# Mean squares of the attention heads by halves of the tokens, and sums of the second weights spread over eight pairs

## The chip, the cores and the metric

The kernel runs on one core of one Trainium2 chip. The metric is the device time of one execution in microseconds (us); before the change the median of three runs is 1240.09 us (1237.65 to 1240.2). A core has TensorE (PE; its weight loads are the rows PEld), VectorE (DVE), ScalarE (ACT), GpSimd (POOL) and SyncE (SP), whose queue issues all DMAs of this kernel in program order.

## What is computed

One layer over 1024 tokens of width 1024 in float32: layer norm, attention without softmax over 8 heads with a decay along the keys, beside it four groups of pooled projections; head outputs are scaled by their root mean square, joined with the pooled groups, projected and added to the residual; then a feed-forward layer of squared ReLU and a per-layer embedding. The part that matters here, in short:

```python
o = o * rsqrt(mean(o * o, per head) + eps) * head_scale   # heads, in pairs
mixed = concat(heads, pooled) ; x = x + mixed @ w_out
h = relu(norm(x) @ w_up) ** 2 ; x = x + h @ w_down
```

## The kernel before

Products of float32 precision are made of three matmuls, high by high, low by high and high by low (L69 to L71); L65 casts to the high part and L66 subtracts for the low one. Tags name the buffers in SBUF that tiles share; a tile that asks for a tag waits until the older tile's last reader is done.

**Attention** goes over 64 tiles: 4 pairs of heads (`pr`) by 2 heads (`j`) by 8 row tiles (`t`). For a tile, `weigh` makes the scores `z` (L396, L397), ACT writes `rr` and `aa` from them, DVE scans (L400), POOL adds (L403); `turn` transposes `aa` (L126), ACT and DVE split it into `ath` and `atl`, and `gather`, after every second tile, multiplies by the values into `o` (L429). `weigh` runs three tiles ahead of `turn`. Between them `fill` puts matmuls of the later projections (`pq`) and of the pooled groups (`pp`), at a rate `RATES[0]` up to tile 48 and `RATES[1]` from it; what is left comes in `fill.finish`. PE's order is the order of the code here; the other engines are ordered by a scheduler.

After the last tile of a pair `rms_square` squares the pair's whole output `oraw` (L441), `rms_stats` multiplies it by `hm` into `pm` (L447), ACT adds eps (L450), POOL raises it to the power of −1/2 (L451) and copies it to `ms` (L453); `rms_apply` transposes a half of it into `pb` (L460) and DVE multiplies `oraw` by it (L462). For pairs 0 to 2 `oraw` is then stored to DRAM (`mspill`); so are pooled groups 5 to 7.

**Out-projection.** `mix(k)` takes the eight inputs in the order 7, 6, 5, 4, 0, 1, 2, 3; six of them come back from `mspill` as `mraw`, 4 is the pooled group in SBUF and 3 the last pair's `oraw`. Each is split and used by the matmuls `acc<-wh,mix`. `wraw` is a row block of `w_out`, `wh` and `wl` its parts, `xr` the residual rows.

**Up stage.** Two hidden blocks make a pair `g`, of 16, computed as two by two blocks with seven products p1 to p7 of 12 matmuls each. Here all engines follow the order of the code, `for g in range(NG)`: p3 of a pair, then p6, p5, p7, and p1 and p2 of the next pair between. `up_load(g, f)` loads half f of the pair's first weights (`uraw`), of which DVE and ACT make sums, highs and lows (`s`, `uh`, `ul`; L574, L655).

The sums of the second weights, for the stage after, are made on the side: `down_fetch(m)` loads two raw blocks of `w_down` (`draw`, 512 KB each), `down_sums(m)` subtracts four times on POOL (L574), `down_out(m)` stores four results of 256 KB (`tspill`). The two buffers are reused, so the loads for m + 1 wait in SP's queue until the stores of m have landed, and stores wait there for the subtractions; all that is queued behind them waits too. `hidden_out` stores the results of the products (`hspill`). Before the change block m was summed at the start of pair g (m = g up to pair 3, g + 1 after it), and stored behind p7, with the loads of m + 1 right after; pair 3 summed and stored block 4 as well, at its end.

Of the kernel before, what the change touches and what calls it, by code (L numbers as in the profile page):

```python
# [8 lines left out]
F32 = mybir.dt.float32  # L9
# [7 lines left out]
P = 128  # L17
# [17 lines left out]
def hymba_layer(ctx: ExitStack, tc: tile.TileContext, x, p, emb_g, emb_b, w_in, attn_g, w_pool,  # L35
# [327 lines left out]
    V.tensor_copy(out=diag[:, S - P:S], in_=ident)  # L363
    oraw = {}

    RATES = (0.37, 0.6)
    AHEAD = 3

    def head_values(pr, j):
# [66 lines left out]
        V.tensor_tensor(out=oraw[k.pr][rows[k.j], (k.t - 1) * P:(k.t + 1) * P],  # L436
                        in0=o[0:HD, 0:2 * P], in1=ob, op=ALU.add)

    def rms_square(pr):
        sq[pr] = slot("ra", "sq")  # L440
        A.activation(out=sq[pr], in_=oraw[pr], func=AF.Square)  # L441

    def rms_stats(pr):

        pm = bank("b6", "pm")[:, 0:2 * NT]
        for i in range(NT):
            T.matmul(pm[:, 2 * i:2 * i + 2], lhsT=sq[pr][:, i * P:(i + 1) * P], rhs=hm,  # L447
                     start=True, stop=True)
        rs = small.tile([P, 2 * NT], F32, name="rms", bufs=2)
        A.activation(out=rs, in_=pm, func=AF.Identity, bias=eps)  # L450
        G.tensor_tensor(out=rs, in0=rs, in1=mhalf, op=ALU.pow)  # L451
        ms[pr] = slot("K", "ms")
        G.tensor_copy(out=ms[pr].rearrange("p (n d) -> p n d", d=HD),  # L453
                      in_=rs.unsqueeze(2).broadcast_to([P, 2 * NT, HD]))

    def rms_apply(pr, c):
        cs = slice(c * CH, (c + 1) * CH)
        pb = bank("b6", "pb")
        for i in range(4):
            T.transpose(pb[:, i * P:(i + 1) * P],  # L460
                        ms[pr][:, (4 * c + i) * P:(4 * c + i + 1) * P], ident)
        V.scalar_tensor_tensor(out=oraw[pr][:, cs], in0=oraw[pr][:, cs],  # L462
                               scalar=osc[:, pr:pr + 1], in1=pb, op0=ALU.mult, op1=ALU.mult)
        if pr < 3 and c:
            load(mspill[pr], oraw[pr])
# [56 lines left out]
    with tc.manual_schedule(engines={mybir.EngineType.PE}):  # L522
        for n in range(-AHEAD, len(tiles)):
            if n >= 0:
                k = tiles[n]
                turn(k)
            if n + AHEAD < len(tiles):
                ahead = tiles[min(n + AHEAD + 1, len(tiles) - 1)]
                if ahead.j == 0 and ahead.t % 4 == 0:
                    fill.until((ahead.pr, ahead.t // 4))  # L530
                weigh(tiles[n + AHEAD])
            fill.rate = RATES[0] if n < 48 else RATES[1]
            if n < 0:
                fill.run(3)
            else:
                fill.share(k.n / P + 1.5)
                if k.t % 2:
                    gather(k)
                for f, *args in later.pop(n, ()):
                    f(*args)  # L540
                if k.j == 1 and k.t == NT - 1:
                    rms_square(k.pr)
                    later.setdefault(n + 2, []).append((rms_stats, k.pr))
                    later.setdefault(n + 8, []).append((rms_apply, k.pr, 0))
                    later.setdefault(n + 10, []).append((rms_apply, k.pr, 1))
        fill.run(4)
        rms_stats(3)
        fill.finish()
        rms_apply(3, 0)
        rms_apply(3, 1)  # L550


    mixh, mixl = {}, {}
# [3 lines left out]
    def mix(k):  # L557
        both = big("mix")
        mixh[k], mixl[k] = both[:, 0:S], both[:, S:2 * S]
        raw = pooled[0] if k == 4 else oraw[3] if k == 3 else None  # L560
        if raw is None:
            raw = slot("K", "mraw")
            load(raw, mspill[k])
        split(raw, mixh[k], mixl[k])
# [375 lines left out]
    def beside(s, n):  # L940
        plan = (PLAN if s else FIRST).get(n, ())
        for what, nx, j, q in plan:
            if s + nx < NS:
                acts[what](s + nx, j, q)

    with tc.manual_schedule(engines=ALL):

        stats, tps = {}, {}
# [89 lines left out]

        for g in range(NG):
            n1, n2 = g + 1 if g + 1 < NG else None, g + 2 if g + 2 < NG else None  # L1040

            m = g if g < 4 else g + 1
            if g:
                up(g, "p6")
                keep(g, "a21")
# [4 lines left out]
                    lows[n1, 0]()  # L1050
            if n1:
                up_load(n1, 1)
                down_sums(m)
            else:
                for i in range(3):
                    fetch_rows(i)
                down_load(0, 1, 0)
# [5 lines left out]
                hidden_out(g - 1, 1)  # L1063
            if n2:
                up_load(n2, 0)
            if not n1:
                down_high(0, 0, 0)
                down_load(0, 1, 1)
# [4 lines left out]
            if g:  # L1073
                hidden_sums(g - 1, 1)
                hidden_out(g - 1, 2)
            if m < NG:
                down_out(m)
            if m + 1 < NG:
                down_fetch(m + 1)
            if not n1:  # L1080
                down_low(0, 0, 0)
                relu2(quarter(g, "a22"))
# [2 lines left out]
            if n1:  # L1085
# [2 lines left out]
                    keep(n1, "a11")  # L1088
                relu2(quarter(g, "a22"))
                up_s21(n1)  # L1090
                if g:
                    up(n1, "p2")
                    take(n1, "a11", "C")
                up_s21_high(n1)
                if not n2:
                    for q in range(2):
                        down_load(0, 0, q)
# [2 lines left out]
            relu2(quarter(g, "a12"), ups[g, "A"])  # L1100
            hidden_out(g, 0)
            hidden_out(g, 3)
            if g == 3:
                down_sums(4)
            if n1:
                if g:
                    relu2(quarter(n1, "a11"))
# [13 lines left out]
            else:  # L1121
# [1 line left out]
                down_high(0, 1, 1)  # L1123
                fetch_rows(3)
                down_load(0, 2, 0)
            if g == 3:
                down_out(4)
                down_fetch(5)

        for s in range(NS - 1):  # L1130
            for n, (name, t) in enumerate(SEQ):
# [200 lines left out]
```

## Time and profile before

| | us |
|---|---|
| median of three runs | 1240.09 |
| profiled execution | 1238.67 |
| its span | 1236.7 |

| engine | busy us | share of the span |
|---|---|---|
| PE | 1163.7 | 94% |
| DVE | 903.1 | 73% |
| ACT | 599.2 | 48% |
| POOL | 520.3 | 42% |

In windows by stretch a row holds the stretch, its length and, for PE, PEld, DVE, ACT and POOL, busy time with the number of instructions; then the granted clock of PE (1.00 is 2.4 GHz, 0.50 is 1.2 GHz), the busy share of the DMA engines and GB/s. A timeline row holds the start, the duration of one or of the grouped instructions together, the engine, line, operation, output<-input, count and, in brackets, idle time before it and who ended it. SPq is SP's queue: a row there is the issue of a DMA, not its transfer.

### The profile page before, as it was taken

How to read it: one execution, taken by the hardware profiler on the slowest of the kernel's cores; microseconds unless marked ns; L12 is line 12 of the kernel's file. 1: busy time of each engine (PE TensorE's matmuls, PEld its weight loads, DVE VectorE, ACT ScalarE, POOL GpSimd, SP SyncE). 2: the span in 40 equal slices, each digit the busy share in tenths (PEclk: the TensorE clock that was granted, in tenths of full speed). 3: DMA queues.
4: the chain of work that ended last, by engine and by line, in shares of the span. 5: the costliest groups of instructions: out<-in, count | busy, mean ns of one | idle time of the engine just before them, and what ended most of it. 6: DMA issues, size and time to landing. Idle time of an engine off the chain costs nothing.

```text
span 1236.7 us, 15529 instructions
## 1 busy us (share of the span) xinstructions
PE 1163.7 (94%) x5520; PEld 964.1 (78%) x5520; DVE 903.1 (73%) x1114; ACT 599.2 (48%) x1038; POOL 520.3 (42%) x368
## 2 busy tenths in 40 slices
PE   7999988899997998699899999999999999998997
PEld 5877877787876876588688888878888888887886
DVE  7735878796865678868576776768888887788565
ACT  5425756675644244454446455466333343335653
POOL 3211443354752236633342332336645564465332
PEclk9999999999997999799899999999999999999999
DMA  9824121121226363378778877799666655643122
GB/s 347 291 115 136 27 61 60 43 60 43 71 83 242 120 243 132 102 253 263 238 256 278 269 252 261 253 378 394 231 220 196 214 175 169 208 138 118 68 78 76
DMA packets 123580, 221.48 MB, mean 179 GB/s; under 512 B 9456, under 2 KB 64240, under 8 KB 123504
## 3 DMA queue, kind: packets, MB, share of 16 engines
q1 hardware_dynamic: 123504, 220.50, 52.4%
q8 instruction: 43, 0.70, 0.2%
q14 instruction: 33, 0.27, 0.1%
HBM read 148.12 MB, written 70.25 MB: 177 GB/s over the span
## 4 chain that ended last, share of the span: by engine, by line
PE 71%; DVE 10%; ACT 6%; DMA 5%; issue 5%; POOL 2%; SPq 1%; DVEq 0%; ACTq 0%; POOLq 0%
PE pd L69 8%; PE pd L71 7%; PE pd L70 7%; PE pu L70 6%; PE pu L71 6%; PE pu L69 6%; PE tp L126 3%; PE pq L69 3%; PE pq L70 3%; PE pq L71 2%; PE acc L70 2%; PE o L429 2%; DVE rr L400 2%; PE acc L71 2%; PE acc L69 2%
## 5 line engine op out<-in xcount | busy, mean ns | idle before, releaser
L574 POOL TENSOR_TENSOR draw<-draw 128x512 f32<-128x512 f32 x64 | 97.1, 1517 | 180.1 <-DMA draw<-in_w_down_dram 177.5
L890 DVE TENSOR_TENSOR xres<-xres,pd 128x512 f32<-128x512 f32 x208 | 137.4, 680 | 45.4 <-PE pd L71 44.5
L574 POOL TENSOR_TENSOR dop<-draw,dop 128x1024 fp32r<-128x1024 f32 (+1 forms) x48 | 112.1, 2355 | 125.2 <-ACT dop L866 107.1
L866 ACT CAST dop<-draw 128x1024 fp32r<-128x1024 f32 (+1 forms) x96 | 81.3, 905 | 134.8 <-DVE xres L890 51.4
L69 PE MATMUL pd<-dop 128*128 128x512 f32 x320 | 125.1, 391 | 2.0 <-DVE xres L890 1.9
L70 PE MATMUL pd<-dop 128*128 128x512 f32 x320 | 124.8, 390 | 0.1
L71 PE MATMUL pd<-dop 128*128 128x512 f32 x320 | 124.6, 389 | 0.0
L574 DVE TENSOR_TENSOR dop<-draw,dop 128x1024 fp32r<-128x1024 f32 (+1 forms) x48 | 85.6, 1784 | 3.6 <-ACT dop L866 3.6
L751 ACT COPY hid<-pu 128x512 f32<-128x512 f32 x48 | 28.2, 588 | 120.8 <-PE pu L71 69.0
L69 PE MATMUL pq<-xh,wh 128*128 128x512 f32 x192 | 77.9, 406 | 0.8 <-DVE ul L66 0.8
L400 DVE TENSOR_TENSOR_SCAN rr<-rr,diag 128x640 f32<-128x640 f32 (+3 forms) x32 | 71.3, 2228 | 9.5 <-ACT rr L398 8.6
L403 POOL TENSOR_TENSOR aa<-aa,rr 128x639 f32<-128x639 f32 (+3 forms) x32 | 56.9, 1779 | 48.4 <-DVE rr L400 48.4
L70 PE MATMUL pq<-xl,wh 128*128 128x512 f32 x192 | 76.7, 399 | 0.0
L71 PE MATMUL pq<-xh,wl 128*128 128x512 f32 x192 | 76.5, 398 | 0.0
L69 PEld LDWEIGHTS pd<-dop 128*128 128x128 f32 x320 | 60.0, 188 | 16.6 <-DVE xres L890 3.2
L574 DVE TENSOR_TENSOR hid<-pu,hid 128x512 f32<-128x512 f32 x48 | 33.0, 688 | 52.7 <-PE pu L71 37.8
L70 PEld LDWEIGHTS pd<-dop 128*128 128x128 f32 x320 | 60.1, 188 | 13.0 <-POOL dop L574 0.8
L71 PEld LDWEIGHTS pd<-dop 128*128 128x128 f32 x320 | 60.1, 188 | 12.5
L65 ACT CAST wh<-wraw 128x1024 fp32r<-128x1024 f32 x36 | 38.0, 1056 | 53.9 <-PE acc L70 26.2
L66 DVE TENSOR_TENSOR atl<-tp,ath 128x512 fp32r<-128x512 f32 (+2 forms) x96 | 50.7, 546 | 15.4 <-ACT ath L65 14.6
L70 PE MATMUL acc<-wl,mix 128*128 128x512 f32 x128 | 51.7, 404 | 4.2 <-POOL wl L66 4.2
L574 DVE TENSOR_TENSOR hid<-hid,hid 128x512 f32<-128x512 f32 x48 | 53.8, 1145 | 0.6
(253 smaller groups left out, 3359.3 us busy)
## 6 DMA issues: line engine op xcount, KB each, us to landing
hspill<-hid SPq DMA_DIRECT2D x48, 512.0 KB, 4.9
draw<-hspill SPq DMA_DIRECT2D x48, 512.0 KB, 6.0
uraw<-in_w_up_dram SPq DMA_DIRECT2D x32, 512.0 KB, 5.8
draw<-in_w_down_dram SPq DMA_DIRECT2D x32, 512.0 KB, 4.7
tspill<-draw SPq DMA_DIRECT2D x64, 256.0 KB, 4.2
wraw<-in_w_out_dram SPq DMA_DIRECT2D x24, 512.0 KB, 3.6
draw<-in_w_down_dram SPq DMA_DIRECT2D x48, 256.0 KB, 5.1
wraw<-in_w_in_dram SPq DMA_DIRECT2D x16, 512.0 KB, 4.9
```

The source lines that it names most:

```text
L65: A.copy(out=h, in_=src)
L66: (eng or V).tensor_tensor(out=l, in0=src, in1=h.bitcast(F32), op=ALU.subtract)
L69: T.matmul(ps, lhsT=lh, rhs=rh, start=start, stop=False, **kw)
L70: T.matmul(ps, lhsT=lh, rhs=rl, start=False, stop=False, **kw)
L71: T.matmul(ps, lhsT=ll, rhs=rh, start=False, stop=stop, **kw)
L126: T.transpose(tp[:, j * P:(j + 1) * P], src[:, (k0 + j) * P:(k0 + j + 1) * P], ident)
L400: V.tensor_tensor_scan(out=rr[:, 0:n][:, ::-1], data0=rr[:, 0:n][:, ::-1], data1=diag[:, S - n:S][:, ::-1], initial=0.0, op0=ALU.mult, op1 ...
L403: G.tensor_tensor(out=aa[:, 0:n - 1], in0=aa[:, 0:n - 1], in1=rr[:, 1:n], op=ALU.mult)
L574: eng.tensor_tensor(out=o, in0=i0, in1=i1, op=op)
L751: A.copy(out=quarter(g, name), in_=ups[g, "A"])
L866: A.copy(out=h, in_=raw)
L890: V.tensor_tensor(out=xres[i][:, cs], in0=xres[i][:, cs], in1=src, op=ALU.add)
```

## The change

There are two edits that share no code. In attention the squares, their means and their use are made by halves of the tokens: half 0 of a pair after row tile 3 of its second head, half 1 after row tile 7, each 1, 2 and 4 tiles later; before, the whole pair was squared at once and its means taken two tiles later, and used eight and ten tiles later. `RATES[1]` goes from 0.6 to 0.8. For the last pair, `mix(3)` splits the two halves apart and applies half 1 just before its split. In the up stage `weight_sums(g, n)` is called at seven steps of every pair: block m is summed at step 6m (up to block 7) or 7(m − 1) and stored, with the next loads, three steps later, so that block 7 is summed at the start of pair 6 and from there the places are as before.

```diff
-    RATES = (0.37, 0.6)
+    RATES = (0.37, 0.8)
...
-    def rms_square(pr):
-        sq[pr] = slot("ra", "sq")
-        A.activation(out=sq[pr], in_=oraw[pr], func=AF.Square)
...
+    def half(c):
+        return slice(c * CH, (c + 1) * CH)
+
+    def rms_square(pr, c):
+        if pr not in sq:
+            sq[pr], ms[pr] = slot("ra", "sq"), slot("K", "ms")
+        A.activation(out=sq[pr][:, half(c)], in_=oraw[pr][:, half(c)], func=AF.Square)
+
+    def rms_stats(pr, c):
+
+        pm = bank("b6", "pm")[:, 0:NT]
+        for i in range(4):
+            T.matmul(pm[:, 2 * i:2 * i + 2], lhsT=sq[pr][:, (4 * c + i) * P:(4 * c + i + 1) * P],
+                     rhs=hm, start=True, stop=True)
...
+        G.tensor_tensor(out=rs, in0=rs, in1=mhalf[:, 0:NT], op=ALU.pow)
+        G.tensor_copy(out=ms[pr][:, half(c)].rearrange("p (n d) -> p n d", d=HD),
+                      in_=rs.unsqueeze(2).broadcast_to([P, NT, HD]))
...
-                if k.j == 1 and k.t == NT - 1:
-                    rms_square(k.pr)
-                    later.setdefault(n + 2, []).append((rms_stats, k.pr))
-                    later.setdefault(n + 8, []).append((rms_apply, k.pr, 0))
-                    later.setdefault(n + 10, []).append((rms_apply, k.pr, 1))
-        fill.run(4)
-        rms_stats(3)
+                if k.j == 1 and k.t in (3, 7):
+                    c = k.t // 4
+                    for m, f in ((1, rms_square), (2, rms_stats), (4, rms_apply)):
+                        later.setdefault(n + m, []).append((f, k.pr, c))
         fill.finish()
-        rms_apply(3, 0)
-        rms_apply(3, 1)
+        for n in sorted(later):
+            for f, *args in later[n]:
+                if f is not rms_apply:
+                    f(*args)
...
+        if k == 3:
+
+            for c in range(2):
+                if c:
+                    rms_apply(3, 1)
+                split(oraw[3][:, half(c)], mixh[k][:, half(c)], mixl[k][:, half(c)])
+            return
...
+    sums_at = {6 * m if m < 8 else 7 * (m - 1): m for m in range(NG)}
+
+    def weight_sums(g, n):
+        n += 7 * g
+        if n in sums_at:
+            down_sums(sums_at[n])
+        if n - 3 in sums_at:
+            m = sums_at[n - 3]
+            down_out(m)
+            if m + 1 < NG:
+                down_fetch(m + 1)
...
-            m = g if g < 4 else g + 1
...
-                down_sums(m)
+                weight_sums(g, 0)
...
-            if m < NG:
-                down_out(m)
-            if m + 1 < NG:
-                down_fetch(m + 1)
+            weight_sums(g, 2)
...
-            if g == 3:
-                down_sums(4)
...
-            if g == 3:
-                down_out(4)
-                down_fetch(5)
+            weight_sums(g, 6)
```

PE's order from the last `z` on, just before the gather of row tiles 60 and 61 to the first `acc`. A triple of `pq` or `pp` is one step of fill. Before, the last gather and what stands behind it:

```order
L429 MATMUL o<-ath,vs 128x256 x7
L429 MATMUL o<-ath,vs 128x128
L429 MATMUL o<-atl,vs 128x128
L429 MATMUL o<-atl,vs 128x256 x7
L69 MATMUL pq<-xh,wh 128x512
L70 MATMUL pq<-xl,wh 128x512
L71 MATMUL pq<-xh,wl 128x512
L69 MATMUL pp<-uh,wph 128x512
L70 MATMUL pp<-ul,wph 128x512
L71 MATMUL pp<-uh,wpl 128x512
...
L447 MATMUL pm<-hm,sq 128x2 x8
L460 MATMUL pb<-ident,ms 128x128 x8
```

and now, with the gather of tiles 60 and 61 ahead of it:

```order
L429 MATMUL o<-atl,vs 128x256 x5
L451 MATMUL pm<-hm,sq 128x2 x4
L126 MATMUL tp<-ident,aa 128x128 x15
L429 MATMUL o<-ath,vs 128x256 x7
L429 MATMUL o<-ath,vs 128x128
L429 MATMUL o<-atl,vs 128x128
L429 MATMUL o<-atl,vs 128x256 x7
L462 MATMUL pb<-ident,ms 128x128 x4
L69 MATMUL acc<-wh,mix 128x512
```

The last fill triple stood three triples behind the last gather and now stands ahead of the gather before it: of the 23 triples behind the last `z` (20 of them ahead of the last gather) 10 are left, and 13 more stand ahead of that `z`. `pm` of half 1 and its `pb` now stand among the `acc` matmuls.

SP's queue at the same place, before:

```order
L74 DMA wraw<-in_w_out_dram 128x1024
L74 DMA mspill<-pooled 128x1024
L74 DMA xr<-xspill 128x1024 x3
L74 DMA mspill<-pooled 128x1024
L74 DMA xr<-xspill 128x1024
L74 DMA uraw<-in_w_up_dram 128x8x128
L74 DMA wraw<-in_w_out_dram 128x1024
L74 DMA mraw<-mspill 128x1024 x6
```

and now:

```order
L74 DMA uraw<-in_w_up_dram 128x8x128
L74 DMA mspill<-pooled 128x1024
L74 DMA wraw<-in_w_out_dram 128x1024
L74 DMA mraw<-mspill 128x1024 x6
L74 DMA xr<-xspill 128x1024 x4
L74 DMA uraw<-in_w_up_dram 128x8x128
```

The six `mraw` loads have passed the four `xr` loads and one `uraw`; one `wraw` still stands right ahead of them.

SP's queue in pairs 2 and 3 of the up stage, from the first half of pair 4's first weights to the second half of pair 5's, before:

```order
L74 DMA uraw<-in_w_up_dram 128x8x128
L74 DMA hspill<-hid_5132 128x1024
L74 DMA tspill<-draw 128x512 x4
L74 DMA draw<-in_w_down_dram 128x1024 x2
...
L74 DMA uraw<-in_w_up_dram 128x8x128
L74 DMA hspill<-hid_5261 128x1024
L74 DMA uraw<-in_w_up_dram 128x8x128
L74 DMA hspill<-hid_5281 128x1024
L74 DMA tspill<-draw 128x512 x4
...
L74 DMA tspill<-draw 128x512 x4
L74 DMA draw<-in_w_down_dram 128x1024 x2
L74 DMA uraw<-in_w_up_dram 128x8x128
```

and now:

```order
L74 DMA uraw<-in_w_up_dram 128x8x128
L74 DMA tspill<-draw 128x512 x4
L74 DMA draw<-in_w_down_dram 128x1024 x2
...
L74 DMA hspill<-hid_5114 128x512
L74 DMA uraw<-in_w_up_dram 128x8x128
L74 DMA tspill<-draw 128x512 x4
L74 DMA draw<-in_w_down_dram 128x1024 x2
L74 DMA hspill<-hid_5295 128x1024
L74 DMA uraw<-in_w_up_dram 128x8x128
...
L74 DMA tspill<-draw 128x512 x4
L74 DMA draw<-in_w_down_dram 128x1024 x2
L74 DMA uraw<-in_w_up_dram 128x8x128
```

The stores of block 2 (with the rows of block 3) have passed one `hspill`; those of block 3 (with block 4's rows) have passed two `hspill` and the `uraw` of pair 5's first half. The stores of block 4 stand where they stood, right ahead of pair 5's second half. Further on only the stores of block 5 move, behind two `hspill`; on the other engines of the up stage nothing but the subtractions moves.

## Rows read from the trace of the kernel before

**Rows 1.** Windows of the up stage by stretch, from one p3 to the next

```profile
586.33:605.37 19.04, 19.04 (x85) 15.77 (x84) 10.71 (x12) 8.87 (x14) 6.71 (x4) 1.00 0.66 221
605.37:633.85 28.48, 22.45 (x86) 17.54 (x85) 17.60 (x20) 10.84 (x16) 10.97 (x8) 0.82 0.86 286
```

**Rows 2.** Timelines of PE, DVE and ACT around the long pair

```profile
588.88 1.99 ACT L655 CAST uh<-uraw 128x1024 fp32r<-128x1024 f32 x2
...
610.80 1.59 DVE L574 TENSOR_TENSOR s<-uraw 128x512 f32<-128x512 f32 x1 [10.12 <-DMA uraw<-in_w_up_dram]
613.15 1.04 ACT L655 CAST uh<-s 128x1024 fp32r<-128x1024 f32 x1 [10.62 <-DVE s L574]
614.25 0.79 PE L69 MATMUL pu<-t2h,uh 128*128 128x512 f32 x1 [5.99 <-ACT uh L655]
```

**Rows 3.** Timeline of SP's queue in pairs 2 and 3

```profile
561.70 0.43 SPq L74 DMA_DIRECT2D uraw<-in_w_up_dram  x1
...
563.56 3.80 SPq L74 DMA_DIRECT2D tspill<-draw  x4
570.92 0.95 SPq L74 DMA_DIRECT2D draw<-in_w_down_dram  x2
...
572.87 0.50 SPq L74 DMA_DIRECT2D uraw<-in_w_up_dram  x1
...
579.65 0.43 SPq L74 DMA_DIRECT2D uraw<-in_w_up_dram  x1
...
588.08 0.91 SPq L74 DMA_DIRECT2D draw<-in_w_down_dram  x2
...
597.86 2.02 SPq L74 DMA_DIRECT2D tspill<-draw  x4
...
603.00 0.38 SPq L74 DMA_DIRECT2D uraw<-in_w_up_dram  x1
```

**Rows 4.** Timeline of POOL in the up stage, subtractions of the second weights

```profile
553.77 2.13 POOL L574 TENSOR_TENSOR draw<-draw 128x512 f32<-128x512 f32 x1 [11.02 <-DMA draw<-in_w_down_dram]
...
592.15 1.81 POOL L574 TENSOR_TENSOR draw<-draw 128x512 f32<-128x512 f32 x1 [10.04 <-DMA draw<-in_w_down_dram]
594.47 5.05 POOL L574 TENSOR_TENSOR draw<-draw 128x512 f32<-128x512 f32 x3 [0.51 <-DMA draw<-in_w_down_dram]
```

**Rows 5.** Windows from late attention into the out-projection, columns as in rows 1

```profile
297.00:346.20 49.20, 48.26 (x280) 41.30 (x279) 37.80 (x47) 33.01 (x80) 32.10 (x29) 1.00 0.20 68
346.20:370.20 24.00, 21.40 (x117) 17.66 (x116) 13.99 (x22) 10.26 (x24) 14.08 (x9) 1.00 0.20 69
370.20:384.60 14.40, 7.30 (x34) 6.08 (x32) 3.79 (x6) 5.73 (x9) 6.30 (x3) 0.66 1.01 345
384.60:388.60 4.00, 3.95 (x10) 3.14 (x11) 3.97 (x5) 3.54 (x4) 0.00 (x0) 0.52 1.02 409
```

**Rows 6.** Timeline of all engines from the last scores to the out-projection

```profile
346.23 0.48 PE L396 MATMUL z<-kh,qs 128*128 128x512 f32 x1
...
369.07 1.16 PE L429 MATMUL o<-atl,vs 128*128 128x128 f32 x8
370.06 0.40 PE L69 MATMUL pq<-xh,wh 128*128 128x512 f32 x1
...
371.81 1.22 DVE L66 TENSOR_TENSOR wl<-wraw,wh 128x1024 fp32r<-128x1024 f32 x1 [0.73 <-DMA xr<-xspill]
...
373.06 2.49 SPq L74 DMA_DIRECT2D wraw<-in_w_out_dram  x1
...
374.49 3.12 PE L447 MATMUL pm<-hm,sq 128*128 128x2 f32 x16
...
375.64 4.15 SPq L74 DMA_DIRECT2D mraw<-mspill  x6
...
378.00 3.38 POOL L451 TENSOR_TENSOR rms<-rms,mhalf 128x16 f32<-128x16 f32 x1 [0.65 <-ACT rms L450]
...
384.65 0.79 PE L69 MATMUL acc<-wh,mix 128*128 128x512 f32 x1
```

More of the change, by code (lines that the diff above doesn't have):

```diff
@@ L437, in gather @@
                         in0=o[0:HD, 0:2 * P], in1=ob, op=ALU.add)
-    def rms_square(pr):
-        sq[pr] = slot("ra", "sq")
-        A.activation(out=sq[pr], in_=oraw[pr], func=AF.Square)
[L443 to L449, printed above, removed]
+    def half(c):
[9 more added lines that the diff above has]
+                     rhs=hm, start=True, stop=True)
+        rs = small.tile([P, NT], F32, name="rms", bufs=2)
         A.activation(out=rs, in_=pm, func=AF.Identity, bias=eps)
[L451 to L454, printed above, removed]
+        G.tensor_tensor(out=rs, in0=rs, in1=mhalf[:, 0:NT], op=ALU.pow)
+        G.tensor_copy(out=ms[pr][:, half(c)].rearrange("p (n d) -> p n d", d=HD),
+                      in_=rs.unsqueeze(2).broadcast_to([P, NT, HD]))
     def rms_apply(pr, c):
-        cs = slice(c * CH, (c + 1) * CH)
         pb = bank("b6", "pb")
@@ L461, in rms_apply @@
                         ms[pr][:, (4 * c + i) * P:(4 * c + i + 1) * P], ident)
-        V.scalar_tensor_tensor(out=oraw[pr][:, cs], in0=oraw[pr][:, cs],
+        V.scalar_tensor_tensor(out=oraw[pr][:, half(c)], in0=oraw[pr][:, half(c)],
                                scalar=osc[:, pr:pr + 1], in1=pb, op0=ALU.mult, op1=ALU.mult)
@@ L559, in mix @@
         mixh[k], mixl[k] = both[:, 0:S], both[:, S:2 * S]
-        raw = pooled[0] if k == 4 else oraw[3] if k == 3 else None
+        if k == 3:
[4 more added lines that the diff above has]
+            return
+        raw = pooled[0] if k == 4 else None
         if raw is None:
@@ L1065, in hymba_layer @@
                 up_load(n2, 0)
+            weight_sums(g, 1)
             if not n1:
@@ L1090, in hymba_layer @@
                 up_s21(n1)
+                weight_sums(g, 3)
                 if g:
@@ L1094, in hymba_layer @@
                 up_s21_high(n1)
+                weight_sums(g, 4)
                 if not n2:
@@ L1102, in hymba_layer @@
             hidden_out(g, 3)
-            if g == 3:
-                down_sums(4)
+            weight_sums(g, 5)
             if n1:
```

## The prediction

> **What bounds the kernel now.** I read the windows by stretch first. In the up stage a pair of hidden blocks is 84 matmuls in 19.04 us, TensorE (PE) busy throughout at a granted clock of 1.00; one stretch is 28.48 us long, with PE busy 22.45 and the clock at 0.82 [rows 1]. So that pair loses 28.48 − 19.04 = 9.44 us. In attention the late stretches are PE-bound too (48.26 us busy of 49.20), but from 346.2 us on PE has gaps, and between the last gather and the first `acc` matmul it is busy 7.30 us of 14.40 at a clock of 0.66, with 0.52 for 4 us more [rows 5]. These two places are what the change can touch, and what ends the waits there comes next.
>
> **The up stall, read backwards.** `p6` of pair 5 waited 5.99 us for ACT's `uh`; that waited for DVE's `s`; that for the DMA of `uraw` [rows 2]. This DMA, the second half of pair 5's first weights, was issued at 603.00 and its matmul began at 614.25: 11.25 us. The same load for pair 4 went out at 572.87, which is 5.58 us behind that pair's stretch start of 567.29; by that pattern 603.00 is 586.33 + 5.58 = 591.9 and so 11.1 us late. In SP's queue it stands behind the sums of the second weights: stores 563.56, next raw rows 570.92 (a hold of 7.36 us); rows 588.08, stores 597.86 (9.78 us for landing and summing), then 5.14 us more to 603.00 [rows 3]. So the pair-3 stretch carries two rounds of sums, one behind the other, and the stall is their chain. PE could have gone on at 614.25 − 5.99 = 608.26. Of the 9.44 us, 5.99 are idle and 3.45 the half-speed clock behind it.
>
> **The seam, read backwards.** From the last `z` (346.23) to the end of the last gather (369.07 + 1.16 = 370.23) pass 24.0 us, of which PE is busy 21.40 with fill. Behind the gather: fill (`pq`, `pp`), then the `pm` matmuls at 374.49, a POOL `pow` of 3.38 us, and the first `acc` at 384.65. The loads `mraw` go out at 375.64, straight behind `wraw` (373.06, released as `wl` ends, 371.81 + 1.22 = 373.03), and the first `acc` follows their issue by 9.0 us [rows 6].
>
> **Part 1: the sums spread out.** No instruction is added or removed; the orders show the three moves on SP. Step by step: the stores of block 2 now come right behind `uraw` (561.70 + 0.43), at 562.2 in place of 563.56. With the hold of 7.36 the rows of block 3 go out at 569.5, their sums are ready for storing 9.78 later, at 579.3, and nothing stands in front of these stores any more but `uraw` of 572.87. The hold of the next stores is bounded by 7.36 and by the last one, 5.14 to the load behind it, of which about 1 is the issue of the rows; I take 4.1, since that round, like the last, finds the queue otherwise empty. So rows of block 4 at 583.4, stores at 593.2, `uraw` at 593.2 + 5.14 = 598.3, and `p6` at 598.3 + 11.25 = 609.6: an idle time of about 1.4 us in place of 5.99, a gain of 4.6. The clock: if it no longer falls, its 3.45 us come back too, 8.0 in all; if it does, 4.6. With the hold at 7.36 `uraw` is at 601.6 and the gain is 1.4. I take 7, with ends of 1.5 and 9.4: 2.6 us of PE idle among 24.0 went with a granted clock of 1.00 in the window from 346.20 [rows 5], so 1.4 us should leave most of it.
> What the move displaces: `hspill` and the first-half `uraw` of pair 5, at 579.29 and 579.65 before, now stand behind the stores of block 3 and the rows of block 4 and go out near 585. ACT casts from that half at 588.88 + 1.0 = 589.9 (the second of two) [rows 2]. The other half took from 603.00 to DVE's first use at 610.80; at 6 to 8 us this one lands at 591 to 593, 1 to 3 us late for ACT. PE is then at `p6` and `p5` of pair 4 with its operands at hand, so I charge 0 to 1. POOL has 4 instructions in this pair, the subtractions themselves [rows 1], so nothing waits behind an earlier sum on POOL. Block 5's stores move behind two `hspill`, costing about 1 us of a queue that by then has the slack of a pair.
>
> **Part 2: mean squares by halves, and the faster rate of fill.** (a) The orders put 13 triples of fill matmuls ahead of the last `z` that stood behind it. A triple is 3 × 19.04/84 = 0.68 us [rows 1], so the last `z` comes 13 × 0.68 = 8.8 us later, at 355.0. (b) Between it and the end of the last gather 20 triples become 10: 24.0 − 6.8 = 17.2 us, which gives 372.2. But fill is what kept PE going through scan, turn, cast and split; without any in the last two tiles some of that chain shows. The gap was 24.00 − 21.40 = 2.6 before, so I add up to 2: the gather ends at 372 to 374, 2 to 4 us later than before, and nothing but the half-0 `pb` stands behind it. (c) `mraw`: it is released through `wl`, whose buffer comes free with the last `pq` triple. That was at 370.06, behind the last gather; now 10 triples follow `z`, the last 2 are `pp`, so `pq` ends near 355.0 + 1.2 + 8 × 0.68 + 1 = 362.6. From the start of the last `pq` triple to `wraw` it took 373.06 − 370.06 = 3.0 (the cast, `wl`), so `wraw` now goes out near 361.9 + 3.0 = 364.9; its issue took 2.49 with `xr` and `uraw` just ahead of it, which the order now has behind `mraw`. `mraw` at 365.3 to 367.4, say 366, and the first `acc` 9.0 later, at 375.0. (d) Before, the first `acc` had also to wait for the squares, `pm`, `pow` and `ms` of the whole pair; now only half 0 stands ahead, ready before the gather, and half 1 stands inside the `acc` matmuls: 3.12/2 = 1.6 us of `pm` and a shorter `pb`, and the chain through POOL's `pow` (3.38 at full width, and no more at half) runs beside some 36 matmuls. Sum: 384.65 − 375.0 = 9.6 gained, less 1.6, plus 0 to 2 of clock, since 4 us at 0.52 and the 0.66 ahead of it need not recur: **9**, with ends of 6 and 11.
> (e) Pairs 0 to 2: the same matmuls in smaller groups; one `pow` of 3.38 becomes two of 1.7 to 3.4 on POOL, so 0 to 3.4 us of POOL a pair. POOL is busy 32.10 of 49.20 us where PE is busy 48.26 [rows 5], so PE hides it: 0, with ±2 for `pm` waiting in PE's fixed order for a square.
>
> **Sum.** −9 − 7 = −16. The profiled execution took 1238.67, 1.4 under the median of 1240.09; on the median, 1240.09 − 16 = 1224.
>
> **Rivals.** R1, the stall mostly stays: the sums' own rounds set the pace, not their place. The subtraction of one form took 2.13 in one pair and 1.81 in another, with 5.05 for the three behind it [rows 4]. If all four take 2.13 (8.52 against 6.86) in two rounds, that is 3.3 us later, and `p6` is at 612.9: a gain of 1.4 to 3. Sum −9 − 3 = −12: **1228**. For it speaks that the sums now run beside other DVE work, against it that no place asks more of POOL. The Trainium skill (SBUF — State Buffer, Who interferes with whom) says that a VectorE instruction with two SBUF inputs and a GpSimd instruction that reads SBUF shut each other out, for a whole instruction; the spread of rows 4 is in keeping with that, and by that rule the rival is likelier in stretches dense with DVE work. R2, the seam gives nothing: `mraw` stays where it was, because `wraw` ahead of it is held by a late cast on ACT or DVE behind the last tiles; the first `acc` is again near 384.65, and only part 1 counts: −7, **1233**. Against it: `wl` waits on nothing but the cast and the last `pq`. R3, slower: fill had been covering the chain of the last tiles, and without it the stretch from the last `z` to the first `acc` stays 384.65 − 346.23 = 38.4 us. It then begins 8.8 later, 1.6 is added inside `acc`, and 7 come back in the up stage: +3.4, **1243**. That decides once this stretch exceeds 37.5 us; my steps give 20. R4, both gains are small (R1 with R2, each at its low end): −2, 1238.
>
> **How the numbers follow.** Forecast 0.62, R1 0.18, R2 0.11, R4 0.04, R3 0.03, and 0.02 for more than 24 us gained. A measurement here tells no difference under 0.2%, 2.5 us. Faster: 0.62 + 0.18 + 0.11 + 0.02 = 0.93; same 0.04 (R4); slower 0.03 (R3). The forecast's own ends are −9.4 − 11 = −20 and, with both terms low, −1.5 − 6 = −7.5. 1216 to 1232 takes in the upper end with 4 us to spare, R1, and the forecast's lower end; R2, R3, R4 and the 0.02 stay out: 0.20.
>
> **What would show it.** Right: the stretch of pair 4 to 5 near 20 to 22 us instead of 28.48, `uraw` issued by 599 rather than 603.00; the six `mraw` issued near 366 and the first `acc` near 375. Wrong: `mraw` still issued after the last gather; PE idle for more than 5 us between the last `z` and that gather; subtractions over 2 us; or a new wait on `uraw`'s first half in pair 4. A loss in the first three attention pairs would speak against (e).

## The result

The changed kernel takes 1230.91 us, median of 8 runs (1228.05 to 1235.88), against 1240.04 us for the kernel before (8 runs, 1237.15 to 1241.53): a ratio of 0.9933, 95% interval 0.9915 to 0.9951. Measured twice more, each time beside the kernel before on one chip, it was 0.9917 (0.9894 to 0.9941) and 0.9920 (0.9902 to 0.9939). So the change gains 8 to 10 us, clearly, where the prediction had 16; the time lies in its range of 1216 to 1232, near the upper end.

The first profile is of an execution of 1235.88 us, the slowest of its eight; two later ones of the same kernel are of 1229.97 and 1228.94 us. They stand beside it below, since one execution alone would mislead.

**The up stage.** Windows of the changed kernel from p3 to p3 (stretch, length, busy us with instructions of PE, PEld, DVE, ACT, POOL, granted clock, DMA share, GB/s), to hold against [rows 1]:

```profile
584.62:604.00 19.38, 19.33 (x85) 15.69 (x84) 9.80 (x11) 8.87 (x14) 8.07 (x6) 1.00 0.82 274
604.00:626.57 22.57, 19.61 (x85) 15.62 (x84) 13.65 (x16) 9.71 (x15) 6.78 (x6) 1.00 0.81 273
626.57:649.60 23.03, 21.20 (x86) 16.76 (x84) 18.61 (x20) 10.86 (x16) 7.98 (x6) 0.93 0.83 278
```

The one long pair of 28.48 us has become two, of 22.57 and 23.03. The waits at their heads, from PE's timeline, to hold against the 5.99 us of [rows 2]:

```profile
609.31 0.50 PE L69 MATMUL pu<-t2h,uh 128*128 128x512 f32 x1 [2.43 <-ACT uh L663]
...
630.75 0.50 PE L69 MATMUL pu<-t2h,uh 128*128 128x512 f32 x1 [1.30 <-ACT uh L663]
```

SP's queue, where [rows 3] had `uraw` of pair 5 at 603.00:

```profile
592.24 1.85 SPq L74 DMA_DIRECT2D tspill<-draw  x4
597.60 0.90 SPq L74 DMA_DIRECT2D draw<-in_w_down_dram  x2
598.60 0.38 SPq L74 DMA_DIRECT2D uraw<-in_w_up_dram  x1
...
600.28 10.97 SPq L74 DMA_DIRECT2D hspill<-hid  x3
611.36 2.77 SPq L74 DMA_DIRECT2D tspill<-draw  x4
616.44 1.10 SPq L74 DMA_DIRECT2D draw<-in_w_down_dram  x2
617.63 0.38 SPq L74 DMA_DIRECT2D uraw<-in_w_up_dram  x1
```

The load of pair 5 (598.60) is 13.98 us behind the start of pair 3's stretch, 584.62; before it was 603.00 − 586.33 = 16.67, and 5.58 would be in time. So it is earlier, as meant, though not in time. And now the load of pair 6, at 617.63, is late in its turn: 13.63 us behind 604.00. Ahead of it stand block 5's stores and block 6's rows, and ahead of those the row of 10.97 us, which holds three `hspill`. The last two of them, the ones that block 5's stores now stand behind, went out only at 610.45. They wait for results that ACT writes to `hid`, and ACT had stood idle in front of the cast for pair 5's late load. POOL, ACT and SP:

```profile
603.31 4.32 POOL L582 TENSOR_TENSOR draw<-draw 128x512 f32<-128x512 f32 x3 [0.85 <-DMA draw<-in_w_down_dram]
...
608.21 1.04 ACT L663 CAST uh<-s 128x1024 fp32r<-128x1024 f32 x1 [7.67 <-DVE s L582]
...
609.79 0.63 ACT L730 ACTIVATE hid<-hid 128x512 f32<-128x512 f32 x1
...
610.45 0.80 SPq L74 DMA_DIRECT2D hspill<-hid  x2
```

Block 5's subtractions were done at 603.31 + 4.32 = 607.63, and its stores went out at 611.36, 3.7 us later. So the first late load delays the second.

**The seam.** A window and then the timeline of the changed kernel, to hold against [rows 5] and [rows 6]:

```profile
370.20:384.02 13.82, 12.07 (x57) 11.28 (x58) 6.81 (x12) 5.61 (x10) 4.24 (x3) 0.54 0.87 331
```

```profile
358.56 0.47 PE L396 MATMUL z<-kh,qs 128*128 128x512 f32 x1
...
367.88 0.49 PE L69 MATMUL pp<-uh,wph 128*128 128x512 f32 x1 [1.31 <-ACT y L496]
...
370.89 0.88 SPq L74 DMA_DIRECT2D mraw<-mspill  x2
...
371.10 0.79 PE L70 MATMUL pp<-ul,wph 128*128 128x512 f32 x1 [2.73 <-DVE ul L66]
...
382.36 1.47 PE L429 MATMUL o<-atl,vs 128*128 128x128 f32 x8
383.67 0.60 PE L462 MATMUL pb<-ident,ms 128*128 128x128 f32 x4
...
384.02 0.48 PE L69 MATMUL acc<-wh,mix 128*128 128x512 f32 x1
```

The last `z` comes 12.3 us later than before and the first `acc` 0.6 earlier, so the stretch between them went from 38.4 to 25.5 us. Behind the last gather nothing is waited for any more: 14.4 us before, 0.2 now. But from the last `z` to the end of that gather it takes 358.56 to 383.83, 25.3 us, where 24.0 stood before and 17 to 19 were forecast. In it PE waits 1.31 and 2.73 us for the last fill triples, and from 370.20 on it is busy 12.07 of 13.82 us at a clock of 0.54: it does its last turns and gathers at half speed. In the two later profiles the waits are the same but less of the stretch runs at the half clock. Windows from the last `z` to the end of the last gather, of the first profile, after_again and after_third:

```profile
358.56:383.83 25.27, 20.39 (x96) 17.61 (x95) 17.41 (x22) 12.13 (x24) 11.70 (x8) 0.73 0.55 200
356.73:380.40 23.67, 18.38 (x96) 15.77 (x95) 17.15 (x22) 12.02 (x24) 12.42 (x8) 0.86 0.57 203
357.19:380.93 23.74, 18.43 (x96) 15.81 (x95) 17.24 (x22) 12.02 (x24) 12.43 (x8) 0.86 0.58 203
```

The marks of all profiled executions (start times on PE in us; the last `z` is the first matmul of the last tile's scores; "pair 4" and "pair 5" are the stretches from that pair's p3 to the next; "stage" is from pair 0's p3 to pair 8's):

| kernel | last `z` | last gather ends | first `acc` | pair 0's p3 | pair 4 | pair 5 | stage |
|---|---|---|---|---|---|---|---|
| before | 346.23 | 370.23 | 384.65 | 529.19 | 28.48 | 19.04 | 161.78 |
| changed, first | 358.56 | 383.83 | 384.02 | 526.80 | 22.57 | 23.03 | 160.88 |
| changed, after_again | 356.73 | 380.40 | 380.59 | 522.58 | 25.92 | 19.04 | 159.20 |
| changed, after_third | 357.19 | 380.93 | 381.12 | 523.70 | 22.02 | 20.12 | 157.15 |
| attn_only | 353.63 | 378.17 | 378.36 | 520.36 | 26.38 | 19.04 | 159.69 |
| halves06 | 346.91 | 372.83 | 386.51 | 529.28 | 29.26 | 19.04 | 162.56 |
| rate08 | 358.21 | 380.82 | 392.47 | 536.23 | 28.76 | 19.04 | 162.96 |
| hold_pp | 356.56 | 379.16 | 389.85 | 531.91 | 21.08 | 21.54 | 156.87 |
| sums_only | 343.22 | 367.24 | 382.64 | 524.38 | 23.20 | 19.04 | 158.02 |
| place_only | 347.70 | 371.74 | 387.28 | 528.94 | 19.04 | 20.81 | 155.62 |
| sums_place | 354.36 | 379.46 | 379.65 | 522.83 | 19.04 | 19.76 | 153.78 |
| sums_place_again | 354.57 | 379.87 | 380.06 | 522.54 | 19.04 | 24.34 | 157.65 |
| place_edge | 354.13 | 378.49 | 378.69 | 520.04 | 19.43 | 25.85 | 159.74 |
| place_r09 | 361.43 | 381.61 | 381.81 | 522.64 | 19.04 | 20.71 | 155.55 |

### The profile page after: what moved, and what is told of

It reads as the page before. It is cut to its first block, busy times and chain, and to the rows that moved or that the text cites. A ratio compares the mean times of both kernels' runs of the same rounds, so it can differ in the third digit from the quotient of the medians.

```text
span 1234.1 us, 15541 instructions
## 1 busy us (share of the span) xinstructions
PE 1168.1 (95%) x5520; PEld 967.6 (78%) x5520; DVE 912.6 (74%) x1115; ACT 600.7 (49%) x1047; POOL 520.9 (42%) x376
## 4 chain that ended last, share of the span: by engine, by line
PE 45%; DVE 6%; DMA 3%; issue 3%; ACT 3%; POOL 1%; DVEq 0%; SPq 0%; POOLq 0%; ACTq 0%
PE pd L69 7%; PE pd L71 7%; PE pd L70 7%; PE pu L71 6%; PE pu L70 6%; PE pu L69 6%; DMA uraw<-in_w_up_dram 3%; PE pg L69 1%; PE pg L71 1%; PE pg L70 1%; DVE s L582 1%; DVE hid L582 1%; DVE ul L582 1%; ACT uh L663 1%; POOL sg L1243 1%
## 5 line engine op out<-in xcount | busy, mean ns | idle before, releaser
L582 POOL TENSOR_TENSOR draw<-draw 128x512 f32<-128x512 f32 x64 | 97.4, 1521 | 175.7 <-DMA draw<-in_w_down_dram 173.1
L65 ACT CAST ath<-tp 128x512 fp32r<-128x512 f32 (+2 forms) x96 | 45.0, 484 | 25.2 <-PE tp L126 24.1
```

The lines of the kernel that those rows point to most:

```text
L65: A.copy(out=h, in_=src)
L582: eng.tensor_tensor(out=o, in0=i0, in1=i1, op=op)
```

## The experiments

Theory: each half of the change gives its gain where the prediction put it, and the shortfall has one cause in each place: in the up stage a second late load, in the seam a wait and the half clock behind it. Rivals: one of the two parts gives nothing, or the gain does not come from its own place.

**The changed kernel again** (no edit).

> The changed kernel itself, to see how much of its profile is the same from run to run. In its first profile the long pair of the up stage (28.48 us before) had become two, of 22.57 and 23.03 us, and the first acc matmul came at 384.02 instead of 384.65. If that is how the change works, and not one odd execution, both show again: two stretches of 22 to 24 us, the first acc between 382 and 386, and a time of 1228 to 1236 us. If the first profile was odd: one stretch near 20.5 us and the first acc near 375, as the prediction had it.

Measured: 1228.82 us, ratio 0.9917 (0.9894 to 0.9941). The pattern is half that of the first profile: one stretch only (25.92, then 19.04), and the first `acc`, at 380.59, is earlier than the 382 to 386 expected. The sum of both pairs is 44.96, against 45.60 in the first.

> The changed kernel once more, beside the next three on one chip: 1228 to 1232. Its long stretches of the up stage have been 22.57 and 23.03 in one profile and 25.92 alone in another; a third profile should sum to the same, 44.5 to 46 us for the two pairs, if the pace of the rounds is fixed and only the pair that it hits differs.

Measured: 1227.31 us, ratio 0.9920 (0.9902 to 0.9939), just under the range expected; 22.02 and 20.12, which is 42.14 and so below the 44.5 expected. What the loads cost is thus not fixed; it depends on the execution. PE's timelines of these two, first after_again and then after_third:

```profile
604.90 0.79 PE L69 MATMUL pu<-t2h,uh 128*128 128x512 f32 x1 [3.28 <-ACT uh L663]
```

```profile
605.38 0.50 PE L69 MATMUL pu<-t2h,uh 128*128 128x512 f32 x1 [1.87 <-ACT uh L663]
```

A wait of 1.87 us made a pair of 22.02 (2.98 lost), one of 3.28 a pair of 25.92 (6.88 lost): the matmul behind it runs 0.79 us in place of 0.50, the mark of the half clock (the granted clock over that pair is 0.87, and 1.00 in the other). About half of that price is the clock.

**Each part alone.** attn_only has the new attention and the old sums, sums_only the old attention and the new sums; their edits are the parts of the diff above.

> Only the half-wise mean squares and the faster rate of fill; the sums of the second weights as before. The prediction's price for this part was 9 us. Theory A (the part gives what the prediction said): 1231. Theory B, from the profile after (the last gather is no earlier, since PE then runs its last two tiles at half clock): the first acc stays within 2 us of 384.65, and the time is 1237 to 1241, with what is gained coming from the clock behind the seam. The up stage keeps its one stretch of 28.5 us in both.

> Only the sums of the second weights spread out; attention as before. The prediction's price for this part was 7 us: 1233, with the pair after the fourth at 20 to 22 us and no other long one. Theory B, from the profile after (the stall is split in two because the stores of block 5 now stand behind two hspill that wait for late results, and the first weights of pair 6 behind them): two stretches that sum to 45 us or so where the old ones sum to 47.5, so a gain of 1 to 3 us, 1237 to 1239.

Measured: attn_only 1231.1 us, 0.9944 (0.9922 to 0.9965), 7 us of 1238.64; sums_only 1236.22 us, 0.9982 (0.9963 to 1.0002), 2 us and not clear of none. Together 9, which is what the change gives: the parts add up. For attn_only both theories miss: the time is A's, but the first `acc` came at 378.36, between the prediction's 375 and B's 382.6; the long stretch was 26.38, not 28.5. For sums_only B's gain of 1 to 3 us is met, but with one stretch of 23.20 us; the second load was in time in that execution. That profile is of one of the fastest of its twelve executions (1231.79 us), so it may show the stage better than it usually is.

**The two edits in attention apart.** halves06 is attn_only with the old rate; rate08 is the kernel before with this line alone:

```diff
-    RATES = (0.37, 0.6)
+    RATES = (0.37, 0.8)
```

> Attention by halves, but the rate of fill left at 0.6; sums as before. If it is the halves that shorten the stretch from the last z to the first acc (only half 0 ahead of acc), most of the gain of attention alone (7.5 us) stays: 1232 to 1235. If it is the rate, the time is that of before, 1237 to 1240, since with fill left over behind the last z both pm and pb of half 1 stand ahead of the first acc again and the stretch is 36 us or more.

> The kernel before with the rate of fill at 0.8 alone; squares of the whole pair. If the rate is what counts: 1231 to 1234. If rate and halves are needed together: the last z comes some 9 us later, the square, pm, pow and pb of the whole pair still stand between the last gather and acc, so the first acc stays at 384 or goes later and the time is 1237 to 1243.

Measured: halves06 1237.79 us, 1.0002 (0.9982 to 1.0023), no gain; rate08 1244.32 us, 1.0053 (1.0029 to 1.0076), 6.6 us slower. Apart they are worth nothing and less than nothing, together 7 us. The window of rate08 from the last `z` to the first `acc`, and PE's timeline in it:

```profile
358.21:392.47 34.26, 22.40 (x110) 19.19 (x109) 15.42 (x22) 12.46 (x25) 14.32 (x8) 0.76 0.51 177
```

```profile
370.72 0.79 PE L70 MATMUL pp<-ul,wph 128*128 128x512 f32 x1 [2.71 <-DVE ul L66]
...
382.82 1.44 PE L447 MATMUL pm<-hm,sq 128*128 128x2 f32 x6 [2.00 <-ACT sq L441]
...
390.85 1.97 PE L460 MATMUL pb<-ident,ms 128*128 128x128 f32 x8 [4.46 <-POOL ms L453]
```

rate08 is slower than the 1243 that was expected at most. With the fill gone, the chain of the whole pair (square, `pm`, `pow`, `pb`) stands bare between the last gather (380.82) and `acc` (392.47). But it is not alone: the six `mraw` stand behind the four `xr` there, and their first cast ends 0.6 us ahead of `acc`, at 390.82 + 1.05 = 391.87:

```profile
382.20 4.36 SPq L74 DMA_DIRECT2D mraw<-mspill  x6
...
390.82 1.05 ACT L65 CAST mix<-mraw 128x1024 fp32r<-128x1024 f32 x1 [4.12 <-DMA mraw<-mspill]
```

In the kernel before, too, both ended together, `pb` at 384.50 and the cast of `mraw` at 384.60, with `acc` at 384.65:

```profile
382.53 1.97 PE L460 MATMUL pb<-ident,ms 128*128 128x128 f32 x8 [4.92 <-POOL ms L453]
383.55 1.05 ACT L65 CAST mix<-mraw 128x1024 fp32r<-128x1024 f32 x1 [5.63 <-DMA mraw<-mspill]
```

In halves06 the fill is still there, behind the last `z`; half 1 then stands ahead of `acc` and the six `mraw` are as late as before, 377.55. What PE waits for at `acc` is `mraw`. The window and PE's timeline:

```profile
346.91:386.51 39.60, 28.15 (x149) 23.55 (x147) 19.48 (x31) 16.48 (x35) 21.30 (x14) 0.86 0.48 167
```

```profile
386.51 0.80 PE L69 MATMUL acc<-wh,mix 128*128 128x512 f32 x1 [2.82 <-ACT mix L65]
```

So the rate moves the fill forward, and the gap that this leaves closes only if both the chain of the mean squares and the six `mraw` leave it. With rate and halves together both do: in attn_only half 1 stands inside the `acc` matmuls, and `mraw` goes out at 365.98, ahead of the `xr`, for the scheduler's order of the queue changed too. No run moves one without the other; by the rows of rate08 either alone would have gained 0.6 us at most. The prediction treated rate and halves as one part and had this right without knowing that either alone would fail.

**The last fill triple held back.** The changed kernel, with the last `pp` triple behind the transposes of tile 62:

```diff
-    fill.add(groups[3][2])
+    last = groups[3][2]
+    fill.add(next(last) for _ in range(1))
...
                 turn(k)
+                if n == 62:
+                    next(last)
...
         fill.finish()
+        next(last, None)
```

> The changed kernel with the last pp triple held back until behind the transposes of tile 62. In all four profiles of the new attention this triple waits 2.7 us for its low part on DVE ahead of the gather of tiles 60 and 61, and PE's clock is halved from there. If that wait is what keeps the stretch from the last z to the end of the last gather at 24 to 25 us, it falls to 17 to 20 us at a clock near 1.00. If it is the chain of DVE, ACT and POOL of the last two tiles, it stays above 23. The order of this kernel puts pm and pb of half 1 ahead of the first acc, which costs at most the 14.4 us of before, so its time is 1226 to 1236 either way; the stretch is the point.

Measured: 1232.61 us, 0.9957 (0.9934 to 0.9980). The stretch is 22.6 us, between the two expectations. The wait for `ul` is gone and another of 2.06 us has come, for the gather's own `atl`; the clock fell again. PE's timeline and a window:

```profile
367.29 1.65 PE L429 MATMUL o<-atl,vs 128*128 128x128 f32 x6 [2.06 <-DVE atl L66]
```

```profile
366.00:379.16 13.16, 10.40 (x49) 9.58 (x50) 7.68 (x12) 3.54 (x8) 4.43 (x4) 0.68 0.40 136
```

So it is not that triple alone: DVE is behind, and whatever PE wants of it next is late. From the last gather to `acc` it takes 10.7 us here, 379.16 to 389.85. That is not the price of half 1 alone, which stands ahead of `acc` in this kernel: its `pb` is done by 386.47, and PE then waits for `mraw`, which is back behind the `xr` loads. SP, PE and ACT:

```profile
380.04 3.39 SPq L74 DMA_DIRECT2D mraw<-mspill  x6
385.36 1.11 PE L462 MATMUL pb<-ident,ms 128*128 128x128 f32 x4 [2.76 <-POOL ms L456]
388.75 1.04 ACT L65 CAST mix<-mraw 128x1024 fp32r<-128x1024 f32 x1 [5.84 <-DMA mraw<-mspill]
389.85 0.80 PE L69 MATMUL acc<-wh,mix 128*128 128x512 f32 x1 [3.38 <-ACT mix L65]
```

**Other places for two blocks.** sums_place is the changed kernel with block 4 stored behind, not ahead of, `uraw` of pair 5, and block 5 ahead of the two `hspill`; place_only is the same on the old attention.

```diff
+    outs_at = {n + {4: 4, 5: 2}.get(m, 3): m for n, m in sums_at.items()}
+
     def weight_sums(g, n):
...
-        if n - 3 in sums_at:
-            m = sums_at[n - 3]
+        if n in outs_at:
+            m = outs_at[n]
```

> The changed kernel, with two blocks stored at another place: block 4 one step later, behind the first weights of pair 5 in SP's queue, and block 5 one step earlier, ahead of the two hspill. If it is the places in the queue that leave the two stretches long, both go to 19 to 20.5 us, and the kernel is 5 to 7.5 us faster than the changed one: 1223 to 1227. If it is the pace of the rounds (loads, subtractions, stores) that sets them, one of the stretches or the next stays above 22 us and the gain is under 3 us.

> Attention as before; the sums spread out, with blocks 4 and 5 stored at the other places. With the changed places alone (sums_only) the gain was 2.4 us. If the up stage's 9.4 us come back in full by the places in the queue, and nothing else eats them: 1229 to 1231, two pairs at 19 to 20 us. If a gain in the up stage is given back later, the stretches are short but the time stays at 1234 or more.

> The changed kernel with the two blocks stored at the other places, once more, on one chip with the changed kernel. The profiles of the up stage say that it is 5 to 7 us faster than the changed one; the two medians of the first comparison said 2.2. If the profiles are right: 1222 to 1225.

Measured: sums_place 1226.62 us, 0.9902 (0.9880 to 0.9924), and again 1227.55 us, 0.9919 (0.9901 to 0.9938), beside 0.9917 and 0.9920 for the changed kernel on the same chips; place_only 1232.29 us, 0.9961 (0.9946 to 0.9976), between its two expectations, against 0.9982 for sums_only on another chip. The first profile showed all that was hoped for, 19.04 and 19.76. The second, slower than the 1222 to 1225 expected, has pair 4 at 19.04, but pair 5 at 24.34. SP's queue and PE's timeline in the two, first sums_place:

```profile
609.39 0.51 SPq L74 DMA_DIRECT2D uraw<-in_w_up_dram  x1
```

```profile
622.53 0.50 PE L71 MATMUL pu<-t2h,ul 128*128 128x512 f32 x1 [0.42 <-DVE ul L582]
```

and sums_place_again, with the window of pair 5:

```profile
610.19 0.49 SPq L74 DMA_DIRECT2D uraw<-in_w_up_dram  x1
```

```profile
623.23 0.50 PE L69 MATMUL pu<-t2h,uh 128*128 128x512 f32 x1 [2.58 <-ACT uh L663]
```

```profile
617.74:642.08 24.34, 21.23 (x85) 16.79 (x84) 17.55 (x20) 12.46 (x19) 6.15 (x5) 0.93 0.86 284
```

Behind the start of pair 4's stretch the load went out 9.7 us in one (609.39 − 599.72) and 11.5 in the other (610.19 − 598.70), and this 1.8 us, with the clock, cost 4.6 us of the pair. So the places do set pair 4 (19.04 to 19.43 in all five profiles with them); for pair 5 the pace of the rounds leaves the load at the edge, and executions fall on both sides (19.76 to 25.85). The two blocks were not moved one at a time, so what each move does alone is not shown. Over all profiles the stage takes 161.75 us on average with the old sums (four), 158.4 with the changed ones (five), 156.5 with the other places (five): gains of 3.3 and 5.3 us. The medians, with 2 and 5 us on the old attention and no clear difference on the new, don't contradict that, but that the other places gain over the changed ones is not shown in time.

**Edge columns on POOL, and a rate of 0.9.** place_edge is sums_place with two small instructions moved from DVE to POOL:

```diff
-        V.tensor_tensor(out=e[:, 0:w - 1], in0=s[:, 0:w - 1], in1=rc[:, 0:w - 1], op=ALU.mult)
+        G.tensor_tensor(out=e[:, 0:w - 1], in0=s[:, 0:w - 1], in1=rc[:, 0:w - 1], op=ALU.mult)
-        V.tensor_tensor(out=d[:, 0:w - 1], in0=e[:, 0:w - 1], in1=y[:, 0:w - 1],
+        G.tensor_tensor(out=d[:, 0:w - 1], in0=e[:, 0:w - 1], in1=y[:, 0:w - 1],
```

> As sums_place, with the edge columns of the pooled groups (L508, L509, 15 columns and fewer) on POOL instead of DVE; PE, ACT and SP keep their order. In the profiles of the new attention the one of 3 columns takes 1.95 us on DVE, where such an instruction takes 0.16, and ends with POOL's multiplication of tile 63; atl of tiles 60 and 61, wl and the low part that the last pp triple waits for stand behind it. If this holds the last tiles up, the wait of 2.73 us falls to about 0.8, the stretch from the last z to the end of the last gather from 24.6 to 19 to 22.5 us, and the kernel is 2 to 5 us faster than sums_place. If the chain of the last tiles bounds the stretch anyway, the wait moves on to the transposes and gathers and the stretch stays above 23.

> The kernel with the two blocks stored at another place, and the rate at 0.9: 3 triples of fill are left behind the last z in place of 10. If PE's own work bounds the stretch from the last z to the first acc, that stretch falls by 7 x 0.68 = 4.8 us and the last z is 4.8 us later: no change, 1225 to 1228. If the chain of the last tiles bounds it, it falls less and the kernel is up to 4 us slower. If the wait for the last low part goes, with the half clock behind it, it is 2 to 5 us faster: 1221 to 1224.

Measured: place_edge 1225.62 us, 0.9905 (0.9889 to 0.9921), the lowest median of all but not clear of sums_place, and at most 2 us faster where 2 to 5 were expected; place_r09 (sums_place with `RATES = (0.37, 0.9)`) 1228.05 us, 0.9919 (0.9887 to 0.9951), the same. In place_edge the wait for `ul` fell from 2.74 to 1.52 us, in the expected direction but not to 0.8. The stretch stayed at 24.4, above the 19 to 22.5 expected and within the 23.7 to 25.3 that it takes without this edit. The theory that this hold sets it is not borne out, but not refuted either, since the hold did not go: it moved to another instruction (last section). PE's timeline and windows:

```profile
365.46 0.80 PE L70 MATMUL pp<-ul,wph 128*128 128x512 f32 x1 [1.52 <-DVE ul L66]
```

```profile
362.00:364.00 2.00, 0.63 (x2) 0.19 (x1) 2.00 (x3) 1.58 (x4) 2.00 (x2) 1.00 0.80 233
364.00:366.00 2.00, 0.54 (x1) 0.50 (x2) 1.41 (x2) 0.00 (x0) 1.21 (x3) 0.60 0.09 30
366.00:368.00 2.00, 2.00 (x10) 1.85 (x9) 0.00 (x0) 0.69 (x1) 0.52 (x1) 0.50 0.99 322
```

PE is busy 0.63 and 0.54 of two windows of 2 us, the clock is 0.50 from 366 on, and from then PE has work all the time: the wait became shorter by 1.2 us, but the half clock behind it came all the same. With the rate at 0.9 the last `z` comes 7 us later and the stretch is 20.2: with 7 triples fewer (4.8 us) it falls by 4.9. That is in keeping with the first of the three expectations, in which PE's own work counts and the sum is no change.

## Why the prediction was right, and where its steps were not

The direction, the two places and the mechanism were right: it is faster by 0.7 to 0.8%, attention gives the larger part, and the order's moves act as read. The size was 16 against 8 to 10. By its steps:

- **(a) 13 triples, the last `z` 8.8 us later.** Right: four profiles with the old rate, on the old attention or halves06, have it at 346.0 on average, the seven with the new attention at 0.8 (without hold_pp) at 355.6, so 9.6.
- **(b) From the last `z` to the end of the last gather 17 to 19 us.** Wrong, and the main miss in the seam: 23.7 to 25.3 in those seven, with 24.0 before. The prediction took 10 triples off at full speed, which leaves PE 21.40 − 6.8 = 14.6 us of work, and allowed for up to 4.6 us of idle time (the 2.6 of before and up to 2 for bare chain). The idle time was near that: 1.31, 2.73 and 0.85 us in the first profile, 25.27 − 20.39 = 4.9 in all, and 5.3 in the two later ones, about the 5 that it had named as a sign of being wrong. What it left out is a second price: the granted clock went to 0.50 behind the waits, for most of the rest in the first profile and for part of it in the later ones, and PE was busy 20.39, 18.38 and 18.43 us. Of that some 0.95 (its length at full clock in halves06) is the `pm` of half 0, which now stands in this stretch; the other 3 to 5 us above 14.6 are, by these rows, the half clock. No run had the stretch at full clock, so this share is worked out and not tested by an edit. In part 1 the prediction had taken rows of 2.6 us idle among 24.0 at a clock of 1.00 as a sign that such gaps are free; those gaps were three, the longest 1.57 us.
- **(c) `mraw` about 11 us behind the last `z`, near 366.** Close: 12.3 us (353.63 to 365.98 in attn_only, 358.56 to 370.89 in the changed kernel). It no longer ends last, since the gather is later still.
- **(d) Nothing left between the last gather and `acc`.** Right: 0.2 us where 14.4 stood. The first `acc` is at 380.4 on average of the same seven against 385.3 of the four with the old rate, 4.9 us where 9.6 were forecast (5.3 by pair 0's p3); what lacks is (b). The charge of 1.6 us for half 1 inside `acc` is not seen: from the first `acc` to the last it takes 100.5 us on average either way.
- **(e) Pairs 0 to 2 at nothing.** Nearly: `pow` of 8 columns takes 1.65 us in the median and 2.42 at the longest, near the lower of its bounds, and (a) leaves 0.8 us. One new wait came, `pb` of pair 1 for POOL's `ms`, 2.59 us:

```profile
247.39 1.11 PE L462 MATMUL pb<-ident,ms 128*128 128x128 f32 x4 [2.59 <-POOL ms L456]
```

- **Part 1, the load of pair 5.** The chain was worked out right: 12.0 us behind the start of pair 3's stretch by the forecast, 11.4, 12.9 and 14.0 in the three profiles, 16.7 before. The idle time at its end, forecast 1.4, was 1.87, 3.28 and 2.43.
- **Part 1, block 5 behind two `hspill`.** This step failed: it was charged "about 1 us of a queue that by then has the slack of a pair". Block 5's stores went out 3.7 us behind the end of its subtractions in all three profiles of the changed kernel, where in sums_place, with no `hspill` ahead, they went out 1.7 us before that end (603.34 against 605.08): some 5 us by these rows. What the prediction did not see is that these `hspill` carry results that ACT writes only behind the cast for pair 5's load, which is still late. And the slack was the stall itself: before, `uraw` of pair 6 went out at 618.76, 13.4 us behind its stretch's start and so about as late as now (13.0 to 14.5), and nothing waited for it, since pair 4 lasted 28.48 us. With the stall gone the next load is late. Of the 7 us taken, 2 (medians) to 3.3 (profiles) came.

Of the rivals, R1 (1228) and R2 (1233) lie on either side of the measured time, but neither is what happened. R1's size for the up stage, 1.4 to 3 us, is about what came, but not by its cause: the subtractions kept their length, 1517 ns a piece before and 1521 after by the pages of the two profiles. That the time still lies in the stated range is partly luck, since the range had been stretched to take in R1 and the forecast's lower end. R2: `mraw` goes out 12.3 us behind the last `z` in place of 29.4, and nothing waits for it, even where the first `acc` is as late as 384.02. R3's stretch of 38.4 us became 24 to 25.5; rate08 alone shows its kind of loss, 34.3 us with the last `z` 12 us later.

What stays open: what the shorter chain and the earlier `mraw` are worth each, and whether the seam could be had at full clock. The three tries (hold_pp, place_edge, place_r09) each left a wait of 1.5 us or more and the half clock behind it.

## What to carry to other kernels

When a stall goes, look at the next user of the same queue: a late load that the stall covered becomes the next stall, and its slack has to be counted from the new, shorter schedule. Ask also what a store in that queue waits for: here it was an engine that itself stood behind the late load. Filler work that is moved forward leaves a gap behind it, and pays only if all that ends in that gap is taken out in the same step, here a chain and a load that ended within 0.6 us of each other; one edit alone can be worth nothing or cost time. A short wait ahead of a dense stretch can be followed by the half clock, as the 2.73 us in the seam were, so price it twice: the wait, and the work behind it at half speed.

## What was not expected of the hardware

A VectorE instruction on 128 x 3 elements took 1.95 us where the same one took 0.15 in the kernel before, and ended with the POOL multiplication that ran beside it (366.36 + 1.95 = 368.31; 365.40 + 2.89 = 368.29). The timelines of the kernel before and of the changed one:

```profile
367.98 0.15 DVE L506 TENSOR_TENSOR e<-s,rc 128x3 f32<-128x3 f32 x1
```

```profile
365.40 2.89 POOL L403 TENSOR_TENSOR aa<-aa,rr 128x1023 f32<-128x1023 f32 x1 [2.19 <-DVE rr L400]
...
366.36 1.95 DVE L508 TENSOR_TENSOR e<-s,rc 128x3 f32<-128x3 f32 x1
```

The Trainium skill (SBUF — State Buffer, Who interferes with whom) says that a VectorE instruction with two SBUF inputs contends with a GpSimd instruction that reads SBUF; the trace agrees, in these 1.95 us. With that instruction moved to POOL the next with two SBUF inputs, `wl`, took 2.09 us in place_edge where it takes 1.21 in the changed kernel, so the hold had only found another victim:

```profile
362.72 2.09 DVE L66 TENSOR_TENSOR wl<-wraw,wh 128x1024 fp32r<-128x1024 f32 x1
```

And the clock: pairs of the up stage with waits of 2.43 and 0.53 us ran at 1.00, one with 2.58 and 0.53 at 0.93; no length of wait divides the two cleanly here, since another with 1.30 and 0.53 was at 0.93 as well.
